# A two-layer diffusion backbone on one core: first modulation by pairs of feature tiles, a re-weighted plan, pages moved by 32 bytes

## The chip, the cores and the metric

The kernel runs on one core of a Trainium2 chip. Its engines are TensorE (PE in the profile; PEld are its weight loads), VectorE (DVE), ScalarE (ACT), GpSimd (POOL) and SyncE (SP), which here issues DMAs only. The metric is the time of one execution on the device in microseconds, as the median of several runs; lower is better.

## The reference

A latent stream x (512 tokens, 1024 features) with a context of 256 tokens passes two layers. Each has a modulated RMSNorm with shift, scale and gate from SiLU(c), a mixer, and an MLP with a squared ReLU. Layer 0 mixes by one input projection, windowed attention beside a bidirectional RWKV-7 recurrence, and an output projection; layer 1 by a Fourier transform and a linear map. Cut to what matters here:

```python
s_lat, s_ctx = silu(c), silu(c_ctx)
for i in range(2):
    sh1, sc1, gt1, sh2, sc2, gt2 = split(s_lat @ ada_w[i] + ada_b[i], 6)
    h = rmsnorm(x, norm1_g[i]) * (1 + sc1) + sh1
    if i == 0:
        csh1, csc1 = split(s_ctx @ ada_w[0] + ada_b[0], 6)[:2]
        hc = rmsnorm(ctx, norm1_g[0]) * (1 + csc1) + csh1
        z, zc = h @ w_in, hc @ w_in
        y = concat(window_attention(z, zc), rwkv_both_directions(z, zc)) @ w_out
    else:
        y = fft2_real(h) @ fourier_w_out
    x = x + gt1 * y
    h = rmsnorm(x, norm2_g[i]) * (1 + sc2) + sh2
    x = x + gt2 * (relu(h @ w1[i]) ** 2 @ w2[i])
return rmsnorm(x, final_g)
```

All of it is in fp32.

## The kernel before, in words

Activations lie with features on the 128 partitions: x is eight tiles of 128 x 512 (x0 to x7), the context eight of 128 x 256 (c0 to c7). A matrix product takes each operand as two fp32r halves, hi and lo = value - hi, and makes three matmuls of them (`mm3`): hi with hi, lo with hi, hi with lo. A weight piece of 128 x 512 is loaded to a page `st`, its hi made by a cast on ScalarE (`whi`), its lo by a subtraction on VectorE (`wlo`).

The stages in order:

- Start. `silu_row` and the lines by it make SiLU of both conditioning vectors (`sT`). The shift and scale of layer 0 come from `adaA` (8 MB of weights) by `arow`: eight matmuls of a 32-column weight tile against 128 x 512 pieces of `adaA`, then a copy to a row and four small matmuls that turn the row into columns. `aab` adds the bias and makes from them AB0: per feature tile two shifts and two scales, for latent and context. `lat(j)` normalises and modulates feature tile j of x (`ht` on VectorE, `hhi` on ScalarE, `hlo` on VectorE) and multiplies it with the first three tiles of `w_in` (`gh`, `gl`), held from the start. `con(j)` does the same for the context (`hchi`, `hclo`).
- Input projection. 20 column tiles of `w_in`, each with its later use (`post`): shift mixing, keys, values, low-rank parts, rotary queries. Results that are wanted in another layout go to DRAM and come back.
- The chain. Six windows of 128 tokens from each side of the recurrence. Each window needs `prep`, `mats` (`ab`, `ed`), `nat`, an inverse of 64 x 64 triangles by 32 x 32 matmuls (`inv`), and then, one after the other, the steps `u`, `s`, `y` (matmuls with `vu`, `zs`, `edl` and the state St). Attention over four blocks (`qry`, `max`, `row`, `attn`) stands between these.
- Output projection (`out`: the attention half, operands mhi and mlo; `read` and the rest: the recurrence half, operands rwhi and rwlo), MLP of layer 0, Fourier layer, MLP of layer 1. An MLP has two halves; each makes 16 hidden tiles from `w1` (operands hhi, hlo) and then eight output tiles from `w2` (operands zhi, zlo, pages `zq` in pool Q). During the first MLP VectorE also reduces the remaining modulation weights `adaB`. The last output tile is made in two halves of 256 tokens, each normalised and stored at once.

The order of the work is not that of the text. All instructions are first recorded by `Plan` with what they read and write. `Plan.solve` then lists them: it goes through time with a cost for each instruction (`Plan.cost`: time that holds the engine, and latency), a priority (longest path behind the instruction plus a lead `ahead`), ring buffers, PSUM banks and the array's tile size; where TensorE would stand idle it puts in `warm` matmuls. `PLAN` is a table of the pieces of the middle part with a lead in us behind the colon. The order that comes out is fixed on every engine by dependencies; each engine then works through its queue in that order. Weight and activation loads are all issued on SP's queue; `dmae` names the queues of the output stores.

Memory pages of a pool lie behind one another in the order of their first use. In pool Q the `wbs` tiles (one float per partition) come ahead of the `zq` pages.

Of the kernel before, what the change touches and what calls it, by code (L numbers as in the profile page):

```python
# [130 lines left out]
def host(inp):  # L131
# [107 lines left out]
class Plan:  # L239
# [97 lines left out]
    def cost(self, r):  # L337
# [354 lines left out]
def body(tc, I, out):  # L692
# [1068 lines left out]
    PLAN = """  # L1761
    tile 0, tile 1:-1.6, post 0, lora 0, tile 2, post 1, lora 1, tile 3:3.8, post 2, lora 2, tile 4, post 3:-1.5,
    lora 3, tile 5, ada 2, post 4, prep 0 0, ada 4:12.8, prep 0 1, tile 6, post 5, mats 0 0, mats 0 1, nat 0 0:-0.2,
    nat 0 1:-11.4, inv 0, tile 7, ada 6:-1.7, post 6, tile 8, ada 8, post 7, ada 10, tile 9, tile 10, ada 12:4.0,
    post 8:25.8, post 9, tile 11:2.0, ada 14, post 10:14.0, tile 12, ada 16, post 11:12.5, rope:4.2, tile 14,
    post 12, prep 1 0, prep 1 1, mats 1 0, mats 1 1, nat 1 0, nat 1 1, tile 15, post 14, inv 1:8.0, tile 16, ada 18,
    post 15, prep 2 0, prep 2 1, mats 2 0, mats 2 1:1.0, nat 2 0, tile 17, ada 20, post 16, tile 18, ada 22, tile 19,
    post 17, inv 2, post 18, ada 24, nat 2 1, tile 13, post 19, post 13, kv:1.9, u 0 0, s 0 0, u 0 1, s 0 1,
    prep 3 0, prep 3 1, u 1 0, s 1 0, mats 3 0, mats 3 1, nat 3 0, nat 3 1, inv 3, qry 0, max 0 0, u 1 1, max 0 1,
    row 0, s 1 1, prep 4 0, bonus 2, prep 4 1, mats 4 0:-29.1, mats 4 1, nat 4 0, nat 4 1, inv 4, ed 2 0:-60.6,  # L1770
    ed 2 1:-32.9, u 2 0, s 2 0:1.9, y 2 0, u 2 1, s 2 1, y 2 1, prep 5 0, prep 5 1:-4.5, mats 5 0, mats 5 1:1.5,
    nat 5 0, inv 5, attn 0, bonus 3, ed 3 0:-32.9, ed 3 1:-32.9, u 3 0, s 3 0, y 3 0, u 3 1, s 3 1, y 3 1, qry 1,
    max 1 0:1.2, max 1 1, row 1, u 4 0, s 4 0, ed 4 0:-32.9, ed 4 1:-32.9, y 4 0, bonus 4:-1.8, u 4 1, attn 1,
    qry 3:-8.8, max 3 0, ed 5 1:-32.9, y 4 1, s 4 1, u 5 0, s 5 0:15.3, ed 5 0:-32.9, max 3 1, row 3:15.2, bonus 5,
    y 5 0:27.2, u 5 1, y 5 1:-4.7, attn 3, qry 2, max 2 0, max 2 1, row 2, attn 2, out 0, out 1:9.5, out 2:-4.9,
    out 3, out 4, out 5, out 6:5.3, out 7, read 4, read 5, read 3, read 2
    """
# [64 lines left out]
    def mlp(l, xs, ai, sh, gt, nxt):  # L1842
# [6 lines left out]
        for f in range(NG):  # L1849
            st = load(I["w1"][l, f])  # L1850
            
            w = split_w(st)
            p = pst("ch" if f < 2 else "iv")
            for k in range(8):
                mm3(p, w, k, us[k], k == 0, k == 7)
            
            pb = pst("rk")
            for k in range(8):
                pe.matmul(pb[:, 0:1], st[k // 4][:, 128 * (k % 4) : 128 * (k % 4) + 128], adv[:, sh + k : sh + k + 1], start=k == 0, stop=k == 7)
            wb = Q.tile([128, 1], F32, tag="wbs", bufs=NG, name="wbs")  # L1860
            act.copy(wb, pb[:, 0:1])
            gs.append((p, wb))
# [270 lines left out]
```

## Time and profile before

| | us |
|---|---|
| median of 3 runs | 1384.6 |
| lowest and highest | 1378.65, 1388.44 |
| the profiled execution's own time | 1379.87 |
| its span in the trace | 1378.1 |
| busy: TensorE, VectorE, ScalarE, GpSimd | 1323.2, 829.3, 616.1, 96.9 |

The span is the time from the first to the last event of the profiled execution; all places in the text (such as 38.80 us) count from its start. A row of the timeline gives start, length, engine, line, operation, what is written and read, and the idle time before it with what ended it. A matmul's length includes its way through the array, so that lengths of neighbours overlap; the rate is read from the starts. A row of a stretch gives its bounds and length, then for TensorE, its weight loads, VectorE, ScalarE and GpSimd the busy time and count, then the granted clock of TensorE (1.00 is full), the share of the DMA engines and GB/s. The clock in the profile's slices is given in tenths. Groups of instructions give the count, the busy time with the mean of one in ns, and the idle time ahead of them. Buffer numbers are left out of names, so `st` stands for every page of that name.

### The profile page before, as it was taken

What the parts mean: (1) busy time and instruction counts of PE and PEld (TensorE: products, weight loads), DVE (VectorE), ACT (ScalarE), POOL (GpSimd) and SP (SyncE); (2) the same over time, 40 slices, a digit from 0 to 9 for tenths busy, and PEclk for the clock granted to TensorE, in tenths of its full rate; (3) what the DMA queues carried; (4) which work ended last, traced back from release to release, by engine and by line L of the source; (5) the groups of instructions that cost most, each with busy time, mean ns of one, the idle gap of its engine ahead of it and who ended that gap; (6) DMA issues with size and microseconds to landing.
All of it is one profiled execution on the core that took longest, in us unless ns stands there. A gap on an engine that the chain in (4) does not pass through costs nothing. (4 is left out here: it accounts for less than half of the span.)

```text
span 1378.1 us, 27531 instructions
## 1 busy us (share of the span) xinstructions
PE 1323.2 (96%) x10811; PEld 1080.5 (78%) x10811; DVE 829.3 (60%) x1730; ACT 616.1 (45%) x1191; POOL 96.9 (7%) x159
## 2 busy tenths in 40 slices
PE   6999999889998999999999999999999999999997
PEld 2888887677857777888887888879988888888876
DVE  2874898788776547776555565675973322333333
ACT  3674754365352335565422454334565522354331
POOL 1420101222011011000000000000000000000000
PEclk9999998889998999999999999999999999999999
DMA  9488985846445213156555565660322322233222
GB/s 364 147 251 259 293 247 137 238 109 182 130 133 156 82 44 112 61 170 197 176 178 181 179 196 170 207 223 14 101 84 92 101 98 92 92 99 98 94 77 77
DMA packets 173938, 204.69 MB, mean 149 GB/s; under 512 B 52008, under 2 KB 87912, under 8 KB 173808
## 3 DMA queue, kind: packets, MB, share of 16 engines
q1 hardware_dynamic: 171920, 200.99, 47.5%
q8 instruction: 85, 1.39, 0.4%
q10 hardware_dynamic: 1376, 1.90, 0.4%
q14 instruction: 45, 0.37, 0.1%
q0 software_dynamic: 512, 0.03, 0.0%
HBM read 177.41 MB, written 25.43 MB: 147 GB/s over the span
## 5 line engine op out<-in xcount | busy, mean ns | idle before, releaser
L683 ACT CAST whi<-st 128x512 fp32r<-128x512 f32 x306 | 187.7, 619 | 446.5 <-PE ps L683 390.3
L683 DVE TENSOR_TENSOR wlo<-st,whi 128x512 fp32r<-128x512 f32 x306 | 207.8, 689 | 228.7 <-ACT whi L683 168.8
L683 PE MATMUL ps<-hhi,whi 128*128 128x512 f32 x616 | 237.7, 396 | 1.6 <-ACT whi L683 1.0
L683 PE MATMUL ps<-hlo,whi 128*128 128x512 f32 x616 | 235.3, 393 | 0.0
L683 PE MATMUL ps<-hhi,wlo 128*128 128x512 f32 x616 | 233.5, 395 | 0.1
L683 PE MATMUL ps<-zhi,whi 128*128 128x512 f32 (+1 forms) x528 | 204.0, 390 | 2.0 <-ACT whi L683 2.0
L683 PE MATMUL ps<-zlo,whi 128*128 128x512 f32 (+1 forms) x528 | 203.3, 390 | 0.0
L683 PE MATMUL ps<-zhi,wlo 128*128 128x512 f32 (+1 forms) x528 | 200.0, 391 | 1.8 <-DVE wlo L683 1.7
L683 PEld LDWEIGHTS ps<-hhi,whi 128*128 128x128 f32 x616 | 116.0, 189 | 27.2 <-ACT whi L683 2.2
L683 PEld LDWEIGHTS ps<-hhi,wlo 128*128 128x128 f32 x616 | 116.1, 189 | 24.0 <-DVE wlo L683 0.6
L683 PEld LDWEIGHTS ps<-hlo,whi 128*128 128x128 f32 x616 | 116.0, 188 | 23.5 <-issue 1.0
L683 PEld LDWEIGHTS ps<-zhi,wlo 128*128 128x128 f32 x528 | 99.3, 189 | 25.7 <-DVE wlo L683 3.3
L683 PEld LDWEIGHTS ps<-zhi,whi 128*128 128x128 f32 x528 | 99.4, 189 | 25.4 <-ACT whi L683 3.1
L683 PEld LDWEIGHTS ps<-zlo,whi 128*128 128x128 f32 x528 | 99.6, 189 | 22.5
L683 POOL TENSOR_TENSOR rs<-ms,pw 128x4 f32<-128x4 f32 (+1 forms) x7 | 7.4, 1063 | 829.3 <-DVE ms L683 829.3
L683 DVE CUSTOM_DVE_ANT_0 st<-st,sB,vec 128x512 f32<-128x512 f32 x56 | 42.0, 750 | 36.1 <-DMA st<-adaB_in 35.9
L683 DVE TENSOR_TENSOR zlo<-s,zhi 128x512 fp32r<-128x512 f32 x64 | 44.2, 692 | 28.5 <-ACT zhi L683 28.4
L683 DVE CUSTOM_DVE_ANT_0 st<-st,sB,adv 128x512 f32<-128x512 f32 x56 | 42.0, 750 | 11.0 <-DMA st<-adaB_in 10.1
L683 ACT ACTIVATE s<-r 128x512 f32<-128x512 f32 x64 | 40.7, 636 | 0.7
L683 PE MATMUL ps<-pr,gq 64*128 64x128 f32 (+1 forms) x384 | 38.7, 323 | 2.2 <-issue 2.2
L683 ACT CAST zhi<-s 128x512 fp32r<-128x512 f32 x64 | 39.6, 621 | 1.4
L683 PEld LDWEIGHTS ps<-pr,gq 64*128 64x128 f32 x384 | 35.0, 225 | 6.6 <-issue 5.5
(395 smaller groups left out, 2297.7 us busy)
## 6 DMA issues: line engine op xcount, KB each, us to landing
st<-w_in SPq DMA_DIRECT2D x256, 256.0 KB, 2.8
st<-adaB_in SPq DMA_DIRECT2D x112, 256.0 KB, 2.9
ada<-adaB_in SPq DMA_DIRECT2D x48, 256.0 KB, 4.6
st<-win_in SPq DMA_DIRECT2D x40, 256.0 KB, 3.8
spl_th<-th SPq DMA_DIRECT2D x16, 384.0 KB, 3.7
pgth<-spl_th SPq DMA_DIRECT2D x24, 256.0 KB, 4.5
st<-adaA_in SPq DMA_DIRECT2D x16, 256.0 KB, 5.0
st<-adaA_in SPq DMA_DIRECT2D x8, 512.0 KB, 7.2
```

The source lines that it names most:

```text
L683: i = getattr(getattr(tc.nc, r.eng), r.op)(*[tr(a) for a in r.args], **{x: tr(a) for x, a in r.kw.items()})
```

## The change

Five things.

First, the layout of `adaA`. Before, its four blocks are the 512 columns of shift 0 to 511, scale 0 to 511, shift 512 to 1023 and scale 512 to 1023; afterwards block q holds 256 columns of shift and the 256 of scale that belong to feature tiles 2q and 2q+1. `aab` runs once per block, over two tiles. The context's norm and its first four tiles (`con`) are recorded between the first four `lat` and the second pair of blocks. The three context sums share two PSUM banks in place of three.

```diff
-    r["adaA"] = np.stack([a0[:, o : o + 512]. ... for o in (0, 1024, 512, 1536)])
+    aq = [np.concatenate([a0[:, 256 * q : 256 * q + 256], a0[:, 1024 + 256 * q : 1280 + 256 * q]], 1) for q in range(4)]
+    r["adaA"] = np.stack([a. ... for a in aq])
...
-    def aab(pt, j, n):
+    def aab(pt, w, j, n=2):
...
     arow(0, pt, pst("ch"), st0[0:8])
     rbx = norm_rows(P0, xs, T, "rk", "op")
+    aab(pt, 0, 0)
     arow(1, pt, pst("ch"), st0[8:16])
-    aab(pt, 0, 4)
+    aab(pt, 1, 2)
...
+            tc.ahead += 10000
             st = loadh(I["win"][m][:, 512 * o : 512 * o + 512])
...
-    gc_ = [pst(t) for t in ("rk", "ch", "ch")]
+    gc_ = [pst(t, (128, 2, 256)) for t in ("rk", "ch")]
...
     for j in range(4):
         lat(j)
+    rbc = norm_rows(P0, cs_, C, "rk", "op", eng=pool)
+    for j in range(4):
+        con(j)
     pt = pst("iv", (128, 2, 4, 2))
     for w in range(2):
         arow(w, pt, pst("rk"), ...)
-    aab(pt, 4, 4)
-    rbc = norm_rows(P0, cs_, C, "rk", "op", eng=pool)
+        aab(pt, w, 4 + 2 * w)
     for j in range(4, 8):
         lat(j)
-    for j in range(8):
+    for j in range(4, 8):
         con(j)
```

Second, the planner's costs of DMA issues and of VectorE, and its starting lead:

```diff
-        self.ahead, self.piece = 56700, 0
+        self.ahead, self.piece = 1700, 0
...
-            return 430.0, 2900.0
+            return 490.0 if r.eng == "sync" else 520.0, 2900.0
...
-            d = 130 + 1.12 * n if n > 64 else 150 + 1.2 * n
+            d = 146 + 1.05 * n if n > 64 else 150 + 1.2 * n
             if r.op == "tensor_scalar" and n > 64:
-                d -= 0.3 * n
+                d += 50 if n <= 256 else 0 if any(self.inps(a) for a in ins) else -0.5 * n
+            if r.op in ("scalar_tensor_tensor", "tensor_tensor_reduce"):
+                d += 62
             if r.op == "tensor_tensor_scan":
-                d += 350
-            return max(d - 83, 55), d
+                d += 530
+            return max(d - (3 if r.op == "tensor_tensor_reduce" else 83), 55), d
```

Third, nearly every piece of `PLAN` has another lead; the order of the pieces in the table is the same. One line of it:

```diff
-    out 3, out 4, out 5, out 6:5.3, out 7, read 4, read 5, read 3, read 2
+    ... out 3:-42.3, out 4:-90.7, out 5:-59.7, out 6:-53.7, out 7:-38.7, read 4:-8.8, ...
```

Fourth, half of the output stores go to GpSimd's queue, and fifth, `wbs` has a third buffer:

```diff
-    dmae = [nc.sync, nc.scalar]
+    dmae = [nc.sync, pool]
...
-            wb = Q.tile([128, 1], F32, tag="wbs", bufs=NG, name="wbs")
+            wb = Q.tile([128, 1], F32, tag="wbs", bufs=3, name="wbs")
```

By the addresses of the built programs this moves the pages behind `wbs` in pool Q (zhi, zlo, the Fourier operands cshi, abhi, u1hi, fwhi and their lo) from byte 0 to byte 32 of a 64-byte line; nearly all other pages, hhi and hlo and the weights among them, are at byte 32 in both.

How the order moves, at three places. In the rows `st` from `adaA_in` are modulation weights (128x512 a piece of the first half, 128x1024 one of the second), `c` the context, `st` from `win_in` the input projection's weights. SP's queue in the first 35 us, before:

```order
L683 DMA st_283<-adaA_in 128x1024
L683 DMA c_297<-cT_in 128x256
L683 DMA st_301<-adaA_in 128x1024
L683 DMA st_311<-adaA_in 128x1024
L683 DMA c_324<-cT_in 128x256
L683 DMA st<-win_in 128x512 x5
L683 DMA sB<-crow_in 128x1024
```

And now the same queue, from the last pieces of the first half on:

```order
L687 DMA st_252<-adaA_in 128x512
L687 DMA st_259<-adaA_in 128x512
L687 DMA st<-win_in 128x512 x4
L687 DMA st_283<-adaA_in 128x1024
L687 DMA st_292<-adaA_in 128x1024
L687 DMA st_303<-adaA_in 128x1024
```

The `w_in` pieces stood behind all of `adaA` and the whole context; four now stand between its halves (a fifth among the x tiles), and the context ahead of it.

TensorE at the first matmuls of `lat` (hhi and hlo against gh and gl; `st,sT` is the first step of `arow`, `cst,row` its last, `warm` the filler), before:

```order
L683 MATMUL ps<-st_301,sT 32x512 x2
L673 MATMUL warm<-identr 128x512 x2
L683 MATMUL ps<-st_311,sT 32x512 x2
L673 MATMUL warm<-identr 128x512 x3
L683 MATMUL ps<-cst,sqa 128x1 x2
L683 MATMUL ps<-hhi,gh 128x512
L683 MATMUL ps<-hlo,gh 128x512
L683 MATMUL ps<-cst,row 128x2 x8
```

Now, first where `lat` begins:

```order
L687 MATMUL ps<-st_259,sT 32x512
L687 MATMUL ps<-cst,rs 128x128 x2
L687 MATMUL ps<-cst,row 128x2 x4
L677 MATMUL warm<-identr 128x512 x2
L687 MATMUL ps<-cst,row 128x2 x4
L677 MATMUL warm<-identr 128x512 x8
L687 MATMUL ps<-hhi,gh 128x512 x3
```

and some 36 matmuls later, where the second half of `adaA` now stands:

```order
L687 MATMUL ps<-hchi,gh 128x256
L687 MATMUL ps<-st_283,sT 32x512 x2
L687 MATMUL ps<-st_292,sT 32x512 x2
L687 MATMUL ps<-st_303,sT 32x512 x2
L687 MATMUL ps<-hclo,gh 128x256
```

`lat` stood behind all four blocks of `adaA`; it now stands behind two, with four feature tiles and the first context tile ahead of the other two.

TensorE at the end of the chain (`edl,vu` and `pr,St` are the step y, `cst,den` and `pT,Vn` attention, `cst,y`, `zg,g`, `cst,vr` and `y,cst` the readout, mhi and mlo the output projection), before, from attention's last products on (the last `edl,vu` stands 18 rows above the first):

```order
L683 MATMUL ps<-pT,Vn 64x512 x2
L683 MATMUL ps<-cst,den 64x128
L683 MATMUL ps<-cst,vr 64x128
L683 MATMUL ps<-cst,den 64x128 x2
L683 MATMUL ps<-cst,vr 64x128
L683 MATMUL ps<-cst,den 64x128
L683 MATMUL ps<-cst,y_7247 128x2 x4
L683 MATMUL ps<-zg,g_7061 128x128 x4
L673 MATMUL warm<-identr 128x512 x5
L683 MATMUL ps<-cst,vr 64x128 x8
L683 MATMUL ps<-y,cst 128x512
L683 MATMUL ps<-mhi,whi 128x512 x2
```

And now, around the last y:

```order
L687 MATMUL ps<-mhi,whi 128x512
L687 MATMUL ps<-mlo,whi 128x512
L687 MATMUL ps<-mhi,wlo 128x512
L687 MATMUL ps<-zs,ab 64x64 x14
L687 MATMUL ps<-mhi,whi 128x512
L687 MATMUL ps<-mlo,whi 128x512
L687 MATMUL ps<-mhi,wlo 128x512
L687 MATMUL ps<-mhi,whi 128x512
L687 MATMUL ps<-edl,vu 64x64 x2
L687 MATMUL ps<-mlo,whi 128x512
L687 MATMUL ps<-mhi,wlo 128x512
L687 MATMUL ps<-edl,vu 64x64 x14
```

Attention's last products and sums stood behind the last y, and the output projection behind them; now both attention and the first output products stand ahead of it. On the whole 71 `warm` matmuls become 46: 19 become 11 in the start, 22 become 6 from there to the end of the chain, 5 become none ahead of the output projection, and the rest stand in the Fourier layer and at the end. Changes of the array's tile size between neighbouring matmuls are 265 before and 282 now. On GpSimd the two stores of the first half of the output stand ahead of the second half's `rs`; on ScalarE no store is left between the end's copies and squares.

More of the change, by code (lines that the diff above doesn't have):

```diff
@@ L173, in host @@
     a0, a1 = f["ada_w"][0], f["ada_w"][1]
-    r["adaA"] = np.stack([a0[:, o : o + 512].reshape(4, 2, 128, 512).transpose(0, 2, 1, 3).reshape(4, 128, 1024) for o in (0, 1024, 512, 1536)])
+    aq = [np.concatenate([a0[:, 256 * q : 256 * q + 256], a0[:, 1024 + 256 * q : 1280 + 256 * q]], 1) for q in range(4)]
+    r["adaA"] = np.stack([a.reshape(4, 2, 128, 512).transpose(0, 2, 1, 3).reshape(4, 128, 1024) for a in aq])
     colT = lambda w, o: w[:, o : o + 128].T
@@ L919, in arow @@
             pe.matmul(pt[:, w, u, :], row[:, 128 * u : 128 * u + 128], K("sel"), start=True, stop=True)
-    def aab(pt, j, n):
+    def aab(pt, w, j, n=2):
         js = slice(j, j + n)
-        dve.tensor_tensor(AB0[:, js, 0:2], pt[:, 0], bc(V(vec, "adb0", j, n), n), ALU.add)
-        dve.tensor_tensor(AB0[:, js, 2:4], pt[:, 1], bc(b1[:, js], n), ALU.add)
+        dve.tensor_tensor(AB0[:, js, 0:2], pt[:, w, 0:2], bc(V(vec, "adb0", j, n), n), ALU.add)
+        dve.tensor_tensor(AB0[:, js, 2:4], pt[:, w, 2:4], bc(b1[:, js], n), ALU.add)
         dve.tensor_tensor(AB0[:, js, 2:4], AB0[:, js, 2:4], bc(V(vec, "n1g0", j, n), n), ALU.mult)
@@ L947, in body @@
             w.append((hi, lo))
+            tc.ahead -= 10000
         wg.append(w)
@@ L956, in body @@
     gl_ = [pst("mm") for m in range(GRP)]
-    gc_ = [pst(t) for t in ("rk", "ch", "ch")]
+    gc_ = [pst(t, (128, 2, 256)) for t in ("rk", "ch")]
     def gctx(m):
-        return gc_[m][:, :C]
+        return gc_[m // 2][:, m % 2, :]
     def lat(j):
@@ L981, in con @@
         for m in range(GRP):
-            mm3(gctx(m), wg[m], j, hc[j], j == 0, j == 7)
+            mm3(gctx(m), wg[m], j, hc[j], j == 0 and m != 1, j == 7 and m != 0)
     for j in range(4):
         lat(j)
+    rbc = norm_rows(P0, cs_, C, "rk", "op", eng=pool)
+    for j in range(4):
+        con(j)
     pt = pst("iv", (128, 2, 4, 2))
@@ L1761, in body @@
     PLAN = """
[L1762 to L1775, printed above, removed]
-    out 3, out 4, out 5, out 6:5.3, out 7, read 4, read 5, read 3, read 2
+    tile 0:9.2, tile 1:-11.4, post 0, lora 0:-0.6, tile 2:12.2, post 1:-15.7, lora 1:-0.6, tile 3, post 2:0.4,
@@ new lines, in body @@
+    lora 2:-0.6, tile 4, post 3, lora 3:-3.3, tile 5, ada 2:21.4, post 4:40.4, prep 0 0:2.5, ada 4, prep 0 1:2.5,
+    tile 6, post 5:-3.3, mats 0 0, mats 0 1, nat 0 0:11.7, nat 0 1, inv 0, tile 7, ada 6:-42.4, post 6, tile 8,
+    ada 8:-0.5, post 7:-14.6, ada 10:-16.1, tile 9, tile 10, ada 12:13.7, post 8, post 9:0.6, tile 11, ada 14:-1.2,
+    post 10:-0.3, tile 12, ada 16:-19.3, post 11, rope:96.2, tile 14, post 12:5.9, prep 1 0:3.4, prep 1 1:2.5,
+    mats 1 0, mats 1 1:-4.0, nat 1 0:1.9, nat 1 1:5.4, tile 15, post 14, inv 1, tile 16:-2.1, ada 18:-3.0, post 15,
@@ new lines, in body @@
+    prep 2 0:15.2, prep 2 1:15.2, mats 2 0:12.7, mats 2 1:12.7, nat 2 0:15.1, tile 17, ada 20, post 16, tile 18,
+    ada 22, tile 19:-5.6, post 17, inv 2, post 18, ada 24, nat 2 1:-5.1, tile 13, post 19:-1.5, post 13:3.2, kv:40.7,
+    u 0 0, s 0 0:1.8, u 0 1, s 0 1:-3.5, prep 3 0:15.3, prep 3 1:-78.4, u 1 0:1.8, s 1 0, mats 3 0, mats 3 1,
+    nat 3 0:-21.8, nat 3 1:-12.4, inv 3, qry 0:-26.3, max 0 0, u 1 1:-4.2, max 0 1, row 0, s 1 1:-12.5,
+    prep 4 0:13.9, bonus 2:0.3, prep 4 1:2.5, mats 4 0, mats 4 1:17.3, nat 4 0, nat 4 1:14.2, inv 4:-6.5,
@@ new lines, in body @@
+    ed 2 0:-30.7, ed 2 1:-44.2, u 2 0:-1.6, s 2 0, y 2 0:-0.1, u 2 1, s 2 1, y 2 1:-3.7, prep 5 0:30.6, prep 5 1:2.5,
+    mats 5 0, mats 5 1, nat 5 0:-0.6, inv 5, attn 0, bonus 3:5.8, ed 3 0:-41.3, ed 3 1:-58.6, u 3 0, s 3 0:-3.0,
+    y 3 0:-2.5, u 3 1, s 3 1, y 3 1:0.9, qry 1:-26.3, max 1 0, max 1 1, row 1, u 4 0:-4.3, s 4 0:-6.1, ed 4 0:-37.2,
+    ed 4 1:-84.6, y 4 0:4.6, bonus 4:31.4, u 4 1, attn 1, qry 3:-45.3, max 3 0, ed 5 1:-15.2, y 4 1, s 4 1:-3.8,
+    u 5 0:-3.8, s 5 0:31.7, ed 5 0:-2.8, max 3 1:-3.8, row 3:7.5, bonus 5:7.5, y 5 0:15.1, u 5 1:13.2, y 5 1:6.6,
@@ L1777, in body @@
+    attn 3:11.3, qry 2:-15.0, max 2 0:8.6, max 2 1:22.6, row 2:10.6, attn 2:13.9, out 0:-21.8, out 1:-28.7,
+    out 2:-45.4, out 3:-42.3, out 4:-90.7, out 5:-59.7, out 6:-53.7, out 7:-38.7, read 4:-8.8, read 5:-11.7,
+    read 3:-11.8, read 2:-1.0
     """
```

## The prediction

> **What bounds the kernel now.** I read the busy times first, then the span cut into stages, then each stage's own rows. The page:
>
> ```profile
> PE 1323.2 (96%) x10811; PEld 1080.5 (78%) x10811; DVE 829.3 (60%) x1730; ACT 616.1 (45%) x1191; POOL 96.9 (7%) x159
> ...
> PEclk9999998889998999999999999999999999999999
> ```
>
> TensorE is busy nearly everywhere, so a saving counts only where its queue gets shorter. The stages, with columns for stretch, length, then busy us and count of TensorE, its weight loads, VectorE, ScalarE and GpSimd, granted clock, DMA share and GB/s:
>
> ```profile
> 0.00:24.00 24.00, 10.44 (x55) 5.31 (x56) 5.73 (x19) 9.42 (x18) 3.68 (x9) 1.00 0.97 347
> 24.00:39.00 15.00, 15.00 (x70) 5.89 (x65) 6.87 (x13) 7.10 (x13) 3.50 (x4) 1.00 1.04 398
> 66.00:200.00 134.00, 132.32 (x865) 111.16 (x864) 100.84 (x224) 83.93 (x174) 18.32 (x29) 1.00 0.88 268
> 200.00:508.00 308.00, 280.16 (x5538) 224.73 (x5537) 223.86 (x571) 134.55 (x291) 44.84 (x90) 0.89 0.50 136
> 508.00:525.00 17.00, 17.00 (x143) 13.43 (x142) 6.18 (x19) 5.65 (x12) 3.34 (x2) 0.80 0.36 102
> 525.00:577.00 52.00, 52.00 (x264) 42.53 (x263) 41.46 (x87) 26.98 (x61) 3.68 (x2) 1.00 0.31 98
> 1100.00:1150.00 50.00, 50.00 (x216) 40.26 (x215) 15.43 (x23) 12.01 (x20) 0.00 (x0) 1.00 0.29 95
> 1200.00:1250.00 50.00, 50.00 (x222) 41.39 (x222) 19.71 (x29) 26.95 (x49) 0.00 (x0) 1.00 0.31 95
> ```
>
> To 39 us loading sets the pace (DMA share about 1). From 66 to 200 us TensorE does. From 200 to 508 us it is a chain of short steps, with the clock at 0.89. The MLPs from 577 us are a stream of matmuls with nothing else near its limit. Each part of the change acts in a different stage.
>
> **The pages at byte 32.** Making `wbs` one buffer larger moves all that follows it in pool Q. By the built programs' addresses, the 34 `zq` pages (zhi, zlo and the Fourier operands) start at byte 0 of 64 before and at byte 32 after; hhi and hlo are at byte 32 in both. TensorE's timeline (start, length) in two stretches, and two groups of instructions:
>
> ```profile
> 1085.00 0.39 PE L683 MATMUL ps<-hhi,whi 128*128 128x512 f32 x1
> 1087.95 0.39 PE L683 MATMUL ps<-hhi,whi 128*128 128x512 f32 x1
> 1110.18 0.40 PE L683 MATMUL ps<-zhi,whi 128*128 128x512 f32 x1
> 1112.75 0.40 PE L683 MATMUL ps<-zhi,whi 128*128 128x512 f32 x1
> L683 PE MATMUL ps<-zhi,whi 128*128 128x512 f32 (+1 forms) x528 | 204.0, 390 | 2.0 <-ACT whi L683 2.0
> ```
>
> From the first row to the second are 13 matmuls, 2.95 us, 226.9 ns each; from the third to the fourth 11, 2.57 us, 233.6 ns. The stretches agree: 50 us hold 222 with hhi (225.2 ns) and 216 with zhi (231.5 ns). Weights, shape and accumulation are alike; what differs is where the moving operand lies. There are 3 x 528 = 1584 such matmuls, of which the last feature tile's 96 run at half width: 1488 x 6.3 ns = 9.4 us. TensorE is the bound there, but part goes into waits for weights that stay where they are, so I take 8.5. If the address is not the cause it is 0; a loss is excluded, since the streams already at byte 32 are the faster ones. The Fourier operands are 256 wide, too few to count.
>
> [...]
>
> **The start.** The modulation weights are regrouped so that two 512-column blocks serve feature tiles 0 to 3, as before, but each gives shift and scale of two tiles; the context and five w_in pieces move ahead of the second half of the weights on SP's queue. Rows of TensorE, ScalarE and VectorE:
>
> ```profile
> 27.91 1.34 PE L683 MATMUL ps<-st,sT 128*32 128x512 f32 x8
> 29.84 1.05 PE L683 MATMUL ps<-st,sT 128*32 128x512 f32 x4
> 37.64 0.96 PE L673 MATMUL warm<-identr 128*128 128x512 f32 x3
> 38.80 0.48 PE L683 MATMUL ps<-hhi,gh 128*128 128x512 f32 x1
> 66.42 0.40 PE L683 MATMUL ps<-hhi,whi 128*128 128x512 f32 x1
> 28.55 0.75 DVE L683 SCALAR_TENSOR_TENSOR ht<-x,AB,rb 128x512 f32<-128x512 f32 x1
> 29.34 0.72 ACT L683 ACTIVATE hhi<-ht,AB 128x512 fp32r<-128x512 f32 x1 [2.03 <-DVE ht L683]
> 30.76 0.74 DVE L683 SCALAR_TENSOR_TENSOR ht<-x,AB,rb 128x512 f32<-128x512 f32 x1
> 37.70 0.69 DVE L683 TENSOR_TENSOR gl<-st,gh 128x512 fp32r<-128x512 f32 x1 [0.24 <-ACT gh L683]
> 37.05 0.62 ACT L683 CAST gh<-st 128x512 fp32r<-128x512 f32 x1 [0.37 <-DMA st<-win_in]
> ```
>
> New first matmul: the order puts the split of the fourth w_in piece ahead of the first `ht` on VectorE. Until then come x 2.10, context 1.05, constants 0.97, sixteen weight blocks 4.19 and five w_in pieces 1.31 MB (sizes from the shapes) = 9.62 MB. 347 GB/s x 24 us brings 8.33; the other 1.29 MB at 398 GB/s take 3.2 us: 27.2 us. About 1.5 us for the landing, 0.62 + 0.69 for the split, 0.3 for AB0, 0.75 + 0.72 for ht and hhi: 31.9 us, 6.9 before today's 38.80. But today's wait is not empty: the second half's modulations stand in it, at the pace of their loads (1.05 us a piece, the gaps filled with warm matmuls). Afterwards they stand among the first real matmuls. Eight pieces cost between 3.5 us (four rows like the 1.34 one, ends overlapped) and 8.4 (1.05 each); their loads have landed, so I take 4.5. From 38.80 to 66.42 are 27.6 us of solid work: 31.9 + 27.6 + 4.5 = 64.0. Feature tiles 0 to 3 come at VectorE's pace (30.76 - 28.55 = 2.2 us against nine matmuls, 2.1 us), and tile 4 now waits for a late row copy and AB0: about 1 us more. 65 against 66.4: 1.5 us gained, between 4 gained and 4 lost. This reaches the end only through 66 to 200 us, where TensorE's queue is full, and I let it.
>
> **The plan.** The costs and leads change no arithmetic, only which work fills which wait. Two waits of the chain stage can be priced (TensorE):
>
> ```profile
> 397.95 4.37 PE L673 MATMUL warm<-identr 128*128 128x512 f32 x15 [0.17 <-DVE ed L683]
> 403.25 1.61 PE L673 MATMUL warm<-identr 128*128 128x512 f32 x5
> 506.46 0.91 PE L683 MATMUL ps<-edl,vu 128*64 128x64 f32 x22
> 521.97 1.41 PE L673 MATMUL warm<-identr 128*128 128x512 f32 x5
> 524.89 1.03 PE L683 MATMUL ps<-mhi,whi 128*128 128x512 f32 x2
> ```
>
> Warm matmuls are what the planner puts where it finds no work. Their 6 us at 398 to 405 us are empty; the new order has none in that place. From the last chain matmul (507.4 us) to the first of the output projection (524.89) 17.5 us pass, because the last attention block must be divided first; VectorE is busy for 6.18 of the 17. In the new order attention ends before the last chain step and the projection starts before it. What then binds is VectorE: from 508 to 577 us it has 6.18 + 41.46 = 47.6 us of work, so of these 69 us at most 21 can go. Half of the 17.5 (9) plus the 6 would be 15. Against it: work that filled the tail now stands inside the chain, and changes of the array's tile size rise from 265 to 282 by the order. I take 6, between 18 gained and 8 lost; corrected VectorE costs differ from the old by 20 ns for most 512-wide rows, too little to count on more.
>
> **The end.** Half of the output stores go from ScalarE's queue to GpSimd's. VectorE, ScalarE, GpSimd, then store rows (count, KB, us to landing):
>
> ```profile
> 1368.14 0.42 ACT L683 ACTIVATE sq<-xn 128x256 f32<-128x256 f32 x1 [2.06 <-DVE o L683]
> 1368.58 0.48 DVE L683 SCALAR_TENSOR_TENSOR o<-xn,vec,rb 128x256 f32<-128x256 f32 x1
> 1369.79 0.70 POOL L683 TENSOR_TENSOR rs<-ms,pw 128x2 f32<-128x2 f32 x1 [5.28 <-DVE ms L683]
> y_out<-o ACTq DMA_DIRECT2D x4, 256.0 KB, 2.4
> q<-mh POOLq DMA_DIRECT2D x8, 2.0 KB, 3.4
> ```
>
> The second `sq` no longer stands behind a store that waits for `o`, but its `ms` stands behind the eight `o` of VectorE (to 1369.06), and `rs` now stands behind two stores on GpSimd: 0.2 us gained. The last store lands 3.4 - 2.4 = 1.0 us later: 0.8 lost, between 0.5 gained and 1.5 lost. [...]
>
> **Sum.** -8.5 - 1.5 - 6 + 0.8 = -15.2. The profiled execution took 1379.87 us (span 1378.1 and 1.8 around it), 4.7 below the median of the three runs: 1364.7 for a like one. The new median is another draw from such a spread, so I add half of the 4.7: 1367.
>
> **Rivals.**
> - The pages do nothing (another property of the z stream slows it, such as its part of memory: zq lies above the others). For: the trace shows no stream at byte 0 in the place of hhi. Against: where hhi and zhi alternate, nothing else differs. 1367 + 8.5 = 1375.5.
> - The chain stage gives back: fuller waits delay the chain itself, 6 gained become 6 lost: 1379. For: 17 more changes of tile size. Against: the stage has 308 us for 280 of overlapped TensorE time.
> - The clock, on the other side. The stage's clock is 0.89 with 22 warm matmuls; the new order has 6. Were it to fall to 0.78, half-speed time would double from 68 to 136 us, and a TensorE-bound stage would grow by 34: 1401. It decides from a clock of about 0.79 (31 us over the forecast is 1% over 1384.6). Against: 20 of the 22 stood in the one wait that is gone. [...]
> - Both waits vanish and VectorE follows: 15 or more gained in the chain, 1356.
>
> **How the numbers follow.** Forecast 0.55 (own range 1358 to 1376), pages idle 0.18, chain gives back 0.12, clock 0.07, more gain 0.08. The range 1352 to 1382 leaves out the clock's case, part of the giving back and the far end of the gain, 0.15. About 1% is what a measurement of this kernel can tell: below 1370.8 lie 0.7 of the forecast, the last case and little of the pages', 0.50; the clock's case is slower, 0.07; between stays 0.43.
>
> **What would show it.** Pages: 50 us of the zhi stream hold 222 matmuls, not 216. Start: first hhi,gh near 32 us, first hhi,whi of 512 near 65. Chain: no long row of warm matmuls, and mhi,whi before the last edl,vu, the stage's clock at 0.89 or above. End: last store's landing near 3.4 us. Wrong if the zhi stream stays at 231 ns, or if the last edl,vu comes later than 510 us.

## The result and the profile after

| | before | changed |
|---|---|---|
| median of 12 runs each | 1377.27 us | 1368.85 us |
| lowest and highest | 1373.85, 1388.44 | 1363.23, 1374.51 |
| the profiled execution (span) | 1379.87 (1378.1) | 1368.63 (1366.6) |

The ratio is 0.9933, with a 95% interval of 0.9911 to 0.9954: faster by 0.67%, clear of zero, and inside the 1% that the forecast set as its bound. The median lies 1.85 us above the forecast 1367, inside the range. The terms behind that number did less well, as the stages show.

The changed kernel's page, busy times and granted clock:

```profile
PE 1311.5 (96%) x10786; PEld 1079.4 (79%) x10786; DVE 831.7 (61%) x1736; ACT 614.3 (45%) x1191; POOL 95.4 (7%) x163
...
PEclk9999998889988999999999999999999999999998
```

TensorE's share is what it was; 11.7 us of its busy time are gone. The same stretches as before, with columns as there:

```profile
0.00:24.00 24.00, 9.52 (x42) 4.59 (x43) 8.55 (x21) 10.75 (x23) 8.00 (x14) 1.00 0.95 329
24.00:39.00 15.00, 15.00 (x69) 8.94 (x66) 8.15 (x17) 5.60 (x10) 0.00 (x0) 1.00 1.04 402
66.00:200.00 134.00, 131.06 (x835) 109.93 (x833) 100.86 (x225) 80.97 (x167) 18.68 (x31) 0.99 0.86 261
200.00:508.00 308.00, 282.77 (x5445) 227.72 (x5445) 225.25 (x573) 136.35 (x296) 43.37 (x90) 0.89 0.50 140
508.00:525.00 17.00, 16.91 (x249) 13.48 (x243) 9.70 (x22) 7.49 (x18) 1.67 (x1) 1.00 0.39 121
525.00:577.00 52.00, 52.00 (x280) 41.91 (x280) 39.46 (x83) 26.36 (x60) 4.94 (x3) 1.00 0.23 78
1100.00:1150.00 50.00, 50.00 (x222) 41.42 (x221) 15.98 (x24) 11.31 (x19) 0.00 (x0) 1.00 0.29 96
1200.00:1250.00 50.00, 50.00 (x223) 41.38 (x222) 19.38 (x28) 27.29 (x49) 0.00 (x0) 1.00 0.31 100
```

The zhi stretch (1100 to 1150 us) holds 222 matmuls, where it held 216. The stretch from 508 to 525 us has its clock back (1.00, was 0.80). But the chain stretch holds fewer matmuls in the same 308 us (5445, was 5538; 16 of the 93 fewer are warm ones) at the same clock of 0.89, and the milestones below show that the chain is later, not earlier. TensorE's timeline at the milestones, and behind it the page's zhi group and its row on the store issues:

```profile
32.91 0.97 PE L687 MATMUL ps<-hhi,gh 128*128 128x512 f32 x3
66.67 0.28 PE L687 MATMUL ps<-hchi,gl 128*128 128x256 f32 x1
...
511.05 0.50 PE L687 MATMUL ps<-mhi,whi 128*128 128x512 f32 x1
515.12 1.04 PE L687 MATMUL ps<-edl,vu 128*64 128x64 f32 x28
574.04 0.39 PE L687 MATMUL ps<-rwhi,wlo 128*128 128x512 f32 x1
```

```profile
L687 PE MATMUL ps<-zhi,whi 128*128 128x512 f32 (+1 forms) x528 | 199.1, 383 | 0.0
...
y_out<-o POOLq DMA_DIRECT2D x4, 256.0 KB, 2.9
```

The first product of `lat` comes at 32.91 us (was 38.80), the last product of the start at 66.67 to 66.95 (was 66.30 to 66.58): six microseconds of head start end in nothing. The output projection starts ahead of the last y, as the order said, but that y now ends at 516.16 us (was 507.37). The last product of the recurrence's half comes at 574.04 (was 575.93). A store lands in 2.9 us on GpSimd's queue.

For what follows, each profiled execution is cut at five such events: the end of the last start product (`hchi,gl` above), the start of the last matmul of rwhi or rwlo ("last rw"), the start of the last matmul of zhi or zlo in the first MLP and of the first one in the second MLP, and the end of the last matmul of all. The runs e1 to e12 are described below. Lengths in us:

| kernel | start | to last rw | first MLP | Fourier layer, half of second MLP | rest of second MLP | behind the last matmul | span |
|---|---|---|---|---|---|---|---|
| before | 66.6 | 509.3 | 363.3 | 150.6 | 281.5 | 6.8 | 1378.1 |
| changed | 67.0 | 507.0 | 356.0 | 153.6 | 274.9 | 8.1 | 1366.6 |
| e1 pages alone | 66.4 | 502.0 | 357.3 | 150.8 | 277.1 | 6.8 | 1360.5 |
| e2 pages back | 68.4 | 508.2 | 359.9 | 151.7 | 279.4 | 8.1 | 1375.8 |
| e3 layout alone | 64.5 | 505.4 | 359.9 | 150.6 | 279.0 | 7.1 | 1366.4 |
| e4 plan alone | 66.8 | 517.7 | 359.8 | 151.7 | 280.1 | 6.8 | 1383.0 |
| e5 layout and pages | 65.1 | 500.9 | 355.8 | 150.8 | 275.2 | 7.0 | 1354.8 |
| e6 queue back | 67.2 | 511.4 | 358.4 | 152.0 | 274.5 | 6.8 | 1370.2 |
| e7 old leads | 67.7 | 523.8 | 358.1 | 153.6 | 275.3 | 8.1 | 1386.6 |
| e8 old costs | 64.5 | 520.6 | 363.5 | 150.9 | 276.9 | 8.1 | 1384.5 |
| e11 old starting lead | 68.3 | 522.1 | 358.9 | 153.5 | 275.6 | 8.1 | 1386.5 |
| e9 weights moved too | 67.3 | 509.1 | 360.0 | 153.2 | 279.3 | 8.1 | 1377.0 |
| e10 mixed offsets | 67.0 | 501.2 | 359.8 | 151.5 | 279.6 | 8.1 | 1367.2 |
| e12 as e5, pages 64 bytes further | 64.9 | 506.9 | 356.8 | 150.4 | 277.7 | 7.0 | 1363.7 |

The second column has to be read with care: before and e1 run the same order up to the first MLP, yet differ there by 7.3 us (their clocks from 200 to 508 us were 0.89 and 0.92). The changed kernel, e2, e6, e9 and e10 have one order there too, and lie between 501.2 (e10, clock 0.91) and 511.4 (e6, 0.87). The other columns repeat to some 2 us for the same order, but for stalls by weights in the MLPs. So small differences in the second column say nothing by themselves; the medians of many runs do.

### The profile page after: what moved, and what is told of

Read it like the earlier page. It is cut to its first block, busy times and chain, and to the rows that moved or that the text cites. A ratio compares the mean times of both kernels' runs of the same rounds, so it can differ in the third digit from the quotient of the medians.

```text
span 1366.6 us, 27500 instructions
## 1 busy us (share of the span) xinstructions
PE 1311.5 (96%) x10786; PEld 1079.4 (79%) x10786; DVE 831.7 (61%) x1736; ACT 614.3 (45%) x1191; POOL 95.4 (7%) x163
## 4 chain that ended last, share of the span: by engine, by line
PE 72%; DVE 2%; issue 2%; DMA 1%; ACT 1%; POOL 0%; SPq 0%; POOLq 0%; DVEq 0%; ACTq 0%
PE ps L687 72%; DMA edd<-ed 0%; PE warm L677 0%; DMA pgr<-spl_r 0%; DMA Minv<-Dg 0%; DMA q<-ml 0%; ACT pgth L687 0%; DVE ab L687 0%; DVE o L687 0%; DVE pT L687 0%; DVE q L687 0%; DVE pgth L687 0%; DVE ed L687 0%; DMA g<-g_in 0%; DVE gq L687 0%
## 5 line engine op out<-in xcount | busy, mean ns | idle before, releaser
L687 PE MATMUL ps<-zhi,whi 128*128 128x512 f32 (+1 forms) x528 | 199.1, 383 | 0.0
L687 PE MATMUL ps<-zlo,whi 128*128 128x512 f32 (+1 forms) x528 | 199.1, 383 | 0.0
L687 PE MATMUL ps<-zhi,wlo 128*128 128x512 f32 (+1 forms) x528 | 195.7, 384 | 1.4 <-DVE wlo L687 1.4
L687 DVE CUSTOM_DVE_ANT_0 st<-st,sB,vec 128x512 f32<-128x512 f32 x56 | 42.0, 750 | 32.2 <-DMA st<-adaB_in 31.8
L687 ACT ACTIVATE r<-ps 128x512 f32<-128x512 f32 x60 | 35.7, 595 | 8.9 <-PE ps L687 8.8
```

The source lines that it names most:

```text
L687: i = getattr(getattr(tc.nc, r.eng), r.op)(*[tr(a) for a in r.args], **{x: tr(a) for x, a in r.kw.items()})
```

## The experiments

"Ratio" is the time to that of the kernel before, run on the same chip, with its 95% interval.

### e1 and e2: the pages alone, and all but the pages

e1, against the kernel before:

```diff
-            wb = Q.tile([128, 1], F32, tag="wbs", bufs=NG, name="wbs")
+            wb = Q.tile([128, 1], F32, tag="wbs", bufs=3, name="wbs")
```

> The kernel before with a third wbs buffer and nothing else, so that the zq pages lie at byte 32 of 64 in the old order. Theory (the address of the moving operand sets the rate): the z streams run 222 to 223 matmuls in 50 us as in the changed kernel, and the time falls by 8.5 us, ratio about 0.994 to the kernel before. Rival (the new order, not the address, made the z streams faster): z streams stay at 216 in 50 us, ratio 1.000. Second rival (the address is all that the change gains): ratio 0.9933, the whole change.

e2 is the same edit undone in the changed kernel (`bufs=NG`).

> The changed kernel with two wbs buffers again, so that the zq pages lie at byte 0 and every instruction order stays that of the changed kernel. Theory: z streams at 216 in 50 us, 8.5 us slower than the changed kernel, ratio about 0.9995 to the kernel before (the other four parts together then gain 1 to 3 us). Rival (order): z streams stay at 222, ratio 0.993.

Measured: e1 0.9945 (0.9917 to 0.9972), median 1368.26 us; e2 1.0017 (0.9995 to 1.0039), median 1377.13. The zhi stretches, e1 then e2:

```profile
1100.00:1150.00 50.00, 50.00 (x222) 41.42 (x221) 14.73 (x22) 11.23 (x18) 0.00 (x0) 1.00 0.30 100
```

```profile
1100.00:1150.00 50.00, 50.00 (x215) 40.22 (x215) 14.81 (x23) 11.18 (x18) 0.00 (x0) 1.00 0.28 94
```

The theory holds: the rate follows the pages, whatever the order. e1 gains 0.55%, 7.6 us of 1376. (Its two MLP columns are 10.4 shorter in the traces; part of that is waits in the first MLP of the kernel before, 363.3 where e3 takes 359.9 with its pages at the same place.) The other four parts together gain nothing: e2 is at 1.0017. That was less than expected (a gain of 1 to 3 us), and the next runs take these parts one by one.

### e3 and e4: the layout alone, the plan alone

e3 is the kernel before with the whole first part of the change (`adaA`, `aab`, `arow` and `con`, `gc_`, the w_in lead) and nothing else. e4 is the kernel before with the costs, the starting lead and the `PLAN` table, and nothing else.

> The kernel before with the new modulation layout, the context ahead of the second half and the earlier w_in pieces, but the old costs, leads, queue and pages. Theory (the second half's matmuls and row steps, moved among the first products, cost what the earlier start brings): first product near 33 us, last one of this stage at 66 to 67 us, ratio 1.000 within 0.002. Rival (an earlier start shows at the end): the stage ends 3 us earlier, ratio 0.998. Second rival (the layout needs the new leads): ratio above 1.003.

> The kernel before with the new costs, starting lead and leads of the plan, but the old layout, queue and pages. Theory (the plan shortens the end of the chain and gives half of it back inside): the recurrence's output products end 2 us earlier than before, ratio 0.9985. Rival (the plan is worth the 6 us forecast for it): ratio 0.9955. Second rival (the leads fit the new layout only): ratio above 1.002, with more warm matmuls in the chain.

Measured: e3 0.9958 (0.9937 to 0.9980), median 1369.78 us; e4 1.0080 (1.0051 to 1.0108), median 1385.61. TensorE in e3 (first and last product of the start, the warm matmuls of the chain), then in e4 (last y, last rw):

```profile
31.10 0.86 PE L685 MATMUL ps<-hhi,gh 128*128 128x512 f32 x3
64.21 0.28 PE L685 MATMUL ps<-hchi,gl 128*128 128x256 f32 x1
378.36 3.47 PE L675 MATMUL warm<-identr 128*128 128x512 f32 x8
```

```profile
525.62 1.04 PE L685 MATMUL ps<-edl,vu 128*64 128x64 f32 x28
584.53 0.39 PE L685 MATMUL ps<-rwhi,wlo 128*128 128x512 f32 x1
```

Both theories were off; of e3's rivals, the one that the earlier start shows at the end came nearest. The layout alone is worth 0.42%, 5.8 us. Its start ends 2.1 us earlier (64.5, before 66.6), and the order that the old plan makes behind it has one short row of warm matmuls (8 in 3.47 us) in place of the two (20 from 397.95 to 404.86 us). These two could make up the 5.8 (2.1 and some 3.5), but the second was not tried by itself. The plan alone loses 0.8%, 11 us: its last y ends at 526.66 us. The second rival, that the leads fit the new layout only, was right on the time; the warm matmuls that it named were not there (three from the start to the last y, where the kernel before has 22).

### e5: layout and pages with the old plan

e3 with the third `wbs` buffer.

> The kernel before with the new modulation layout and the third wbs buffer; costs, leads and store queue stay old. Theory (pages and layout act in different stages and add up, the new plan is what gave the rest back): ratio 0.9945 x 0.9958 = 0.990 to the kernel before, some 4 to 5 us below the changed kernel. Rival (the layout's gain was its new order falling luckily against the slow z streams): ratio 0.9945, that of the pages alone. The last y near 503 us, the z streams at 222 in 50 us.

Measured: 0.9875 (0.9854 to 0.9897), median 1359.51 us. This kernel beats the one before and the changed one; its interval ends below that of the changed kernel (0.9911 to 0.9954). The gains add up, as expected, and a little better. Its start, last y and last rw:

```profile
64.79 0.28 PE L685 MATMUL ps<-hchi,gl 128*128 128x256 f32 x1
498.06 0.91 PE L685 MATMUL ps<-edl,vu 128*64 128x64 f32 x22
565.96 0.39 PE L685 MATMUL ps<-rwhi,wlo 128*128 128x512 f32 x1
```

e3 and e5 differ in the pages only, and the two MLP columns give what they are worth: 359.9 to 355.8 and 279.0 to 275.2, 7.9 us. e2 and the changed kernel are the same pair in the new order: 3.9 + 4.5 = 8.4 us.

### e6: the stores' queue

```diff
-    dmae = [nc.sync, pool]
+    dmae = [nc.sync, nc.scalar]
```

> The changed kernel with the second half of the output stores on ScalarE's queue again. Theory: the last store lands 1 us sooner and rs no longer stands behind stores, 0.5 to 1.5 us faster than the changed kernel, ratio 0.9925 to the kernel before. Rival (the new queue is what costs the 8 us that the changed kernel loses on the sum of its layout and pages): ratio 0.988, with the loss visible after 1340 us of its trace. Second rival: no difference, 0.9933.

Measured: 0.9925 (0.9904 to 0.9946), the changed kernel 0.9933: by time alone no difference can be told. The traces tell it: behind the last matmul 6.8 to 7.1 us pass in every kernel with ScalarE's queue, and 8.1 in every one with GpSimd's. GpSimd's rows at the end, of the changed kernel and then of e6:

```profile
1356.22 0.74 POOL L687 DMA_DIRECT2D y_out<-o  x1 [0.60 <-DVE ms L687]
1356.98 0.72 POOL L687 TENSOR_TENSOR rs<-ms,pw 128x2 f32<-128x2 f32 x1
1362.05 0.72 POOL L687 DMA_DIRECT2D y_out<-o  x1 [0.66 <-DVE o L687]
```

```profile
1361.97 0.69 POOL L687 TENSOR_TENSOR rs<-ms,pw 128x2 f32<-128x2 f32 x1 [5.18 <-DVE ms L687]
```

The last issue starts 0.3 us behind the last `o` (0.03 in e6), a store lands in 2.9 us (2.3 in e6), and some 0.4 more passes behind the landing, for a reason that no row names: 1.3 us. Ahead of the last matmul, `rs` starts 1.0 us behind its `ms` in place of 0.08, because a store stands in between, but that `ms` comes 0.6 us sooner behind the last z matmul (3.57 us, 4.14 in e6): 0.4 us more. So the queue costs 1.7 us, and it isn't what ate the gains.

e5 and e6 differ in the plan alone (costs, starting lead, leads): 0.9925 / 0.9875 = 1.0051, some 7 us, with intervals that don't overlap. TensorE's chain in both, e5 first: `edl,vu` is a window's y, `vu,ab` begins the u of a later one, `pT,Vn` is attention.

```profile
431.72 0.99 PE L685 MATMUL ps<-edl,vu 128*64 128x64 f32 x28
...
443.32 0.95 PE L685 MATMUL ps<-edl,vu 128*64 128x64 f32 x24
...
452.26 0.98 PE L685 MATMUL ps<-vu,ab 128*64 128x64 f32 x26
```

```profile
430.54 1.10 PE L687 MATMUL ps<-edl,vu 128*64 128x64 f32 x32
452.13 1.28 PE L687 MATMUL ps<-pT,Vn 128*64 128x512 f32 x4
455.38 1.08 PE L687 MATMUL ps<-pT,Vn 128*64 128x512 f32 x4
...
463.69 1.70 PE L687 MATMUL ps<-vu,ab 128*64 128x64 f32 x26
...
519.65 1.03 PE L687 MATMUL ps<-edl,vu 128*64 128x64 f32 x28
578.57 0.39 PE L687 MATMUL ps<-rwhi,wlo 128*128 128x512 f32 x1
```

Up to the y at 431 us the two are level. Then e5 has its next y 11.6 us later and a further u at 452; in e6 attention comes in between, the next u waits until 463.7, and the last y ends at 520.68 in place of 498.97. What the new order gets for it is a shorter tail: from the last y to the last rw 57.9 us in e6 (519.65 + 1.03 to 578.57) against 67.0 in e5. In these two traces it saves 9 behind the last y and pays 22 ahead of it. But e5's profiled run is the shortest of its six and e6's the longest, so 22 is too much. With the new layout, the last y ends at 499.0 to 506.3 us under the old plan (e3, e5, e12) and at 510.3 to 520.7 under the new one (changed, e2, e6, e9, e10): the means are 14.2 us apart, the means of the tails 8.6. By these traces the plan loses 5.6 us up to the last rw.

### e7, e8 and e11: parts of the plan undone in the changed kernel

e7 has the old `PLAN` table. e8 has the old costs and the old starting lead (more lines of the cost rule go back with those shown):

```diff
-        self.ahead, self.piece = 1700, 0
+        self.ahead, self.piece = 56700, 0
...
-            return 490.0 if r.eng == "sync" else 520.0, 2900.0
+            return 430.0, 2900.0
...
-            d = 146 + 1.05 * n if n > 64 else 150 + 1.2 * n
+            d = 130 + 1.12 * n if n > 64 else 150 + 1.2 * n
...
```

e11 has the first of these lines alone.

> The changed kernel with the old leads of PLAN; costs, starting lead, layout, queue and pages stay new. Theory (the new leads put attention and the output projection ahead of the last windows, whose y so comes 9 to 14 us later, and the tail behind it shrinks by only about 8): last y back to 503 to 508 us, 5 to 8 us faster than the changed kernel, ratio 0.988 to 0.990. Rival (the costs or the starting lead carry the loss): ratio 0.993, last y still near 515.

> The changed kernel with the old costs of DMA issues and VectorE and the old starting lead; leads, layout, queue and pages stay new. Theory (the leads carry the loss): ratio 0.993 or, since leads tuned for other costs fit worse, up to 1.000; last y at 515 us or later. Rival (costs or starting lead carry the loss): ratio 0.988 to 0.990, last y near 505.

> The changed kernel with the old starting lead of 56700; costs, leads, layout, queue and pages stay new. Theory (the new starting lead lets input projection work in among the first products, which makes the start 2 us longer than with the old plan): last product of the start at 65 us, not 67, 2 us faster than the changed kernel, ratio 0.992. Rival (the costs make the start longer): start to 67 us as before, ratio 0.993. Second rival (the leads were fitted to the starting lead): ratio 0.998 or above.

Measured: e7 1.0036 (1.0014 to 1.0059), e8 1.0054 (1.0033 to 1.0074), e11 1.0060 (1.0030 to 1.0089). All three theories failed on the time; that leads and costs which don't belong together fit worse was named for e8 (too small, up to 1.000) and was e11's second rival, which came true. Whichever part of the plan goes back, the kernel gets 1% slower than the changed one, and each time above all in the same column: 521 to 524 us from the start to the last rw, the five kernels with the whole plan 501 to 511. (e8 also has 363.5 in the first MLP, with seven warm matmuls there.) The granted clock goes along with some of it: over all runs its mean is 0.971 in the changed kernel, 0.966 in e7 and 0.965 in e11, and whether that is a cause of their time or comes of their waits isn't shown. e8 has 0.971 too, and there the clock explains nothing. The leads were fitted to these costs, this starting lead and (by e4) this layout; taken apart they are worse than the old plan. So the 7 us belong to the plan as a set, and which of its leads puts attention there isn't settled.

Two smaller prices can be given to the costs. First, the start: with the new layout it ends at 64.5 to 65.1 us in e3, e5, e8 and e12 (old costs) and at 67.0 to 68.4 in the changed kernel, e2, e6, e7, e9, e10 and e11 (new costs). e11 differs from e8 in the costs alone and has 68.3 to its 64.5, so the theory on the starting lead fell. Second, the Fourier layer, where the old costs put 14 warm matmuls and take 150.4 to 150.9 us with the MLP's half, and the new ones 20 and 151.5 to 153.6. Rows of it, e5 then changed:

```profile
980.69 2.57 PE L675 MATMUL warm<-identr 128*128 128x512 f32 x10
```

```profile
980.78 2.70 PE L677 MATMUL warm<-identr 128*128 128x512 f32 x11
991.04 1.75 PE L677 MATMUL warm<-identr 128*128 128x512 f32 x7
```

### e9, e10 and e12: what about the address

e9, against the changed kernel, moves everything behind `AB0` by 32 bytes, and the zq pages by 32 more:

```diff
-    AB0 = const.tile([128, 8, 4], F32, name="AB0")
+    AB0 = const.tile([128, 8, 5], F32, name="AB0")
...
-            wb = Q.tile([128, 1], F32, tag="wbs", bufs=3, name="wbs")
+            wb = Q.tile([128, 1], F32, tag="wbs", bufs=4, name="wbs")
```

> The changed kernel with everything behind AB0 moved by 32 bytes (AB0 one column wider) and a fourth wbs buffer: hhi, hlo, gh, whi, wlo, mhi and rwhi now at byte 0 of 64, zhi and zlo still at byte 32, instruction orders as in the changed kernel. Theory (the moving operand's own start decides): the hhi streams take 233 ns a matmul, 216 in 50 us, the zhi streams stay at 227 with weights at byte 0; 1848 MLP products and some 200 others at 512 wide cost 6.3 ns each, 10 to 13 us in all, ratio about 1.001 to the kernel before. Rival (a moving operand on another offset than the weights is what is slow): hhi streams stay at 227 and zhi streams fall to 233, ratio 1.000. Second rival (the high part of the memory was slow at byte 0, the low part isn't): both stay at 227, ratio 0.993.

e10 makes the hidden tiles' pages 64 bytes longer and places the tiles at eight offsets in them:

```diff
+    ZO, zn = (0, 4, 8, 12, 1, 2, 6, 14), [0]
...
+        o = ZO[(zn[0] // 2) % 8]
+        zn[0] += 1
+        return Q.tile([128, 528], dt, tag="zq", bufs=34, name=name)[:, o : o + 512]
```

> The changed kernel with zhi and zlo pages 64 bytes longer and each hidden tile put at another place in its page: pair by pair 32, 48, 0, 16, 36, 40, 56 and 24 bytes past a multiple of 64. Theory A (only a start at byte 0 of 64 is slow): 227 ns at all offsets but 0, 233 there, z streams near 220 in 50 us. Theory B (only byte 32 is fast): 233 at all others. Theory C (the rate depends on the offset in several steps): something below 226 ns at one of them.

e12 is e5 with `bufs=5`.

> The kernel with the new layout and old plan, its zq pages 64 bytes further than in the run with layout and pages (five wbs buffers): zhi and zlo at byte 96 of 128, the weights and hhi at byte 32 of 128; order unchanged. Theory (moving operand and weights must start at the same byte of 64): z streams at 227 ns, 222 in 50 us, ratio 0.9875 as with 64 bytes less. Rival (they must agree to 128 or 256 bytes): z streams at 233 ns, 216 in 50 us, ratio 0.994 to 0.996.

The zhi stretch and the hhi stretch of e9, then the zhi stretch of e10, then of e12:

```profile
1100.00:1150.00 50.00, 50.00 (x216) 40.16 (x215) 15.42 (x23) 11.89 (x20) 0.00 (x0) 1.00 0.28 95
1200.00:1250.00 50.00, 50.00 (x222) 41.42 (x221) 19.58 (x29) 26.95 (x49) 0.00 (x0) 1.00 0.29 95
```

```profile
1100.00:1150.00 50.00, 50.00 (x216) 40.35 (x215) 15.30 (x23) 10.88 (x18) 0.00 (x0) 1.00 0.29 95
```

```profile
1100.00:1150.00 50.00, 50.00 (x220) 41.02 (x219) 15.40 (x24) 11.07 (x19) 0.00 (x0) 1.00 0.29 95
```

e9 turns the picture over. Its hhi pages are at byte 0 and run at 222; its zhi pages are at byte 32 and run at 216. The forecast's byte 32 is not it; the first rival is right for these streams: they are slow where the moving operand starts at another byte than the weights, which e9 moved to 0. The time agrees: 0.9982 (0.9952 to 1.0012) at a rival's 1.000. Put together, by the mean distance of the starts of neighbouring 512-wide matmuls in the MLPs (distances over 260 ns, the waits, left out; addresses from the built programs):

| | moving operand, byte of 64 | weights, byte of 64 | mean ns |
|---|---|---|---|
| before, hhi and hlo | 32 | 32 | 226.8 |
| before, zhi and zlo | 0 | 32 | 233.3 |
| changed, zhi and zlo | 32 | 32 | 226.9 |
| e9, hhi and hlo | 0 | 0 | 226.9 |
| e9, zhi and zlo | 32 | 0 | 233.3 |
| e12, zhi and zlo (64 bytes further) | 32 | 32 | 229.2 |
| e10, zhi and zlo, all | eight places | 32 | 232.7 |
| e10, those at byte 32 alone | 32 | 32 | 231.6 |

e12 adds that agreeing to 64 bytes is not all: with 64 bytes between them modulo 256 (in the changed kernel 0) the mean is 229.2, between the two. Its time, 0.9911 (0.9880 to 0.9941), is 0.36% or 5 us above e5's, with intervals that overlap; 2.3 ns x 1488 = 3.4 us would be the share of the pages. e10, with offsets mixed from tile to tile, ran at 232.7 ns on average and at 231.1 to 235.7 by offset: all three of its theories were about the moving operand alone, and none fits. Its one time was 1369.26 us. The rule from e9 doesn't fit e10 either: the 170 matmuls whose moving operand starts at the weights' byte took 231.6 ns there, hardly less than the rest. So the rule describes streams in which every tile starts at the same place; what sets the pace of a single matmul stays open. In e9 the weights moved together with all else but the pages of pool Q, so that it is the weights and not another operand is the plainest reading (its rows, such as `ps<-zhi,whi`, name just these two as read), not shown by itself.

## Why the prediction was right, and where its steps were not

- **The pages (-8.5).** Right in size: 7.9 and 8.4 us by stages, 7.6 by the ratio of e1. The rate after the change, 222 matmuls in 50 us, was called. The cause as put ("where the moving operand lies") was half of it: what counts for a stream is where it lies relative to the weights (e9: 226.9 ns at the weights' byte, 233.3 ns 32 bytes from it), and e10 shows that this isn't the whole rule (231.6 ns at the weights' byte). The rival that the pages do nothing is out.
- **The start (-1.5).** For the layout alone the step held: first product at 31.1 us (31.9 forecast; its terms as listed add up to 31.8, and the 1.5 us for the landing among them is a guess that no row here shows by itself: the rows give the time from issue to landing, in the median 3.8 us for a piece of `win_in` before and 4.0 in the changed kernel), start shorter by 2.1 (e3). In the whole change it is longer by 0.4. What failed is that the plan was costed at nothing here: "corrected VectorE costs differ from the old by 20 ns for most 512-wide rows, too little to count on more". The costs order the start too, and take 2 to 3 us of it. The first 512-wide hhi,whi came at 69.31 us, not near 65; as a sign it was ill chosen, because 21 narrow products of the input projection now stand between the start's last product and it (17 in e3, which has it at 66.37). The price of the second half among the products was also low, as TensorE's rows in the changed kernel show:

```profile
42.97 1.91 PE L687 MATMUL ps<-st,sT 128*32 128x512 f32 x12
...
45.72 1.05 PE L687 MATMUL ps<-st,sT 128*32 128x512 f32 x4
...
50.30 1.92 PE L687 MATMUL ps<-st,sT 128*32 128x512 f32 x16
...
53.09 0.95 PE L687 MATMUL ps<-cst,row 128*128 128x2 f32 x8
```

  The first three hold the path for some 4.7 us (from a row's start to that of the next product); the last and two like it of four matmuls each, which the sum had left out, for 1.5 more. That is 6.2 us, where the forecast had 4.5.
- **The plan (-6).** Wrong in sign. On the new layout the set costs 0.5% (e6 against e5), some 7 us: about 2.6 in the start and 1.8 in the Fourier layer (means of the columns, the five kernels with the whole plan against e3, e5 and e12), the rest in the chain. The step that failed is "Half of the 17.5 (9) plus the 6 would be 15": the stretch behind the last y did shrink, by 9 us up to the last rw, and the warm rows did go, but the work that filled them stands ahead of the last windows' steps, and on that layout the last y comes later by 14. The case "chain stage gives back" named this; it was given 0.12. The text had its own alarm, the last y later than 510 us, and it went off.
- **The layout behind the start.** No term stood for it. With the old plan the new layout gained 5.8 us, of which the start explains 2.
- **The end (+0.8).** 1.7 us by the traces of e6 and the changed kernel. The landing was 2.9 us, not 3.4, so less than forecast, but the later issue and the time behind the landing, which had no term, make 1.3 of it. The 0.2 us that the sum had as gained through `ms` and `rs` are 0.4 lost.
- **The clock.** Still 0.89 in the chain, with 68 us at 0.50 in both traces, and with six warm matmuls from the start to the last y in place of 22: the slower rival didn't come.

The sum was -15.2 us; the profiled runs differ by 11.2 and the medians by 8.4. That the total came near is luck: a gain that wasn't seen (the layout's) stood against a loss that wasn't seen (the plan's), the sum was some 7 us too large, and the base that it was taken from was 5 us too high, because the kernel before has a median of 1377.27 us over twelve runs, 7 below that of the three that the forecast had (1384.6).

## What to carry to other kernels

Before a kernel that streams matmuls is tuned further, look at the start addresses of its moving operands and of its weights: where they differed modulo 64 bytes, one spare buffer was worth 0.55% here, and nothing else had to change. A table of leads belongs to the costs and the code that it was fitted with; change one and the table has to be made anew, and each part of such a change is to be timed alone, since here the parts that looked like one improvement were two gains and a loss. When a planner fills a wait in front of a chain's last step, check on the trace whether that step itself moved: a shorter tail behind a later step is no gain.

## What the runs showed of the hardware that was not expected

- The rate of a stream of 512-wide fp32r matmuls went with the start of the moving operand relative to the weights: 227 ns at the same byte (changed kernel), 229 at 64 bytes apart modulo 256 (e12), 233 at 32 apart (before, e9). Where the start changes from tile to tile (e10), the matmuls at the same byte took 231.6 too.
- One and the same program varies by 0.8%, and the clock that it is granted goes along: the twelve runs of the changed kernel go from 1363.23 us at a mean clock of 0.976 to 1374.51 at 0.967, and two kernels with the same order in the chain took 502.0 and 509.3 us there. The chain's rows from 200 to 508 us, of e1:

```profile
200.00:508.00 308.00, 278.71 (x5589) 222.86 (x5589) 222.29 (x573) 133.61 (x290) 45.82 (x91) 0.92 0.50 138
```

Before, the same stretch of the same order had 0.89 and 5538 matmuls. In the traces of the kernel before and of the changed one the clock has two values, 1.00 and 0.50, and changes on a grid. Three stretches of the changed kernel:

```profile
416.40:419.80 3.40, 3.40 (x57) 3.28 (x52) 0.62 (x2) 1.02 (x3) 0.00 (x0) 0.50 0.44 130
419.80:426.60 6.80, 5.40 (x251) 4.94 (x252) 3.06 (x12) 0.95 (x2) 0.00 (x0) 1.00 0.48 129
426.60:430.00 3.40, 3.40 (x68) 3.28 (x66) 2.01 (x5) 0.36 (x1) 0.00 (x0) 0.50 0.27 30
```

In both traces every stretch at 0.50 (11 before, 13 in the changed kernel) lasts 3.41 us or a whole multiple of it, up to 13.65 us (the one at the very end is cut off), and within a trace all begin on one grid of 3.41 us. Against the span's start this grid lies differently: at 2.67 us past a multiple of 3.413 us before, at 3.37 us in the changed kernel. From 200 to 508 us the stretches at 0.50 add up to 51 us in e1 and 68 in the kernel before; in the one order of the changed kernel, e2, e6, e9 and e10 they add up to between 58 (e10) and 78 (e6). Whether the place of the grid is what makes one program's time vary, no run here shows.
